# A two-layer decoder trunk on one core: the order of all engines' work laid by a timing model inside the kernel, in place of fixed distances

## The chip, the core and the metric

The kernel runs on one core of a Trainium2 chip. The core has a matrix engine (PE, with its weight loads shown as PEld), a vector engine (DVE), a scalar engine (ACT), a general engine (POOL), and a sync engine (SP) that issues most transfers. The metric is the device time of one execution in microseconds (us), as the median of several runs; lower is better.

## The reference, cut to what matters

Two layers over 256 tokens of width 1024, all in float32. Each layer is a half-step gated feed-forward (FFN) of inner width 2816, a token mixer beside a 4-head attention to 256 memory tokens, and a second half-step FFN; a last norm ends it. Layer 0's mixer is a causal pooling over windows of 2, 4, 8 and 16 tokens, layer 1's a differential attention with 8 heads.

```python
for i in range(2):
    kv = mem_n @ mem_w_kv[i]
    x = x + 0.5 * swiglu(rmsnorm(x, norm_g[i, 0]), ffn_w_up[i, 0], ffn_w_down[i, 0])
    h = rmsnorm(x, norm_g[i, 1])
    x = x + (pool_layer if i == 0 else diff_layer)(h, ..., mem_k, mem_v)
    x = x + 0.5 * swiglu(rmsnorm(x, norm_g[i, 2]), ffn_w_up[i, 1], ffn_w_down[i, 1])
return rmsnorm(x, final_norm_g)
```

## The kernel before

Every float32 product is made of three matmuls (`mm3`, L271): each operand is split into a rounded `hi` and a remainder `lo`, and hi*hi, hi*lo and lo*hi are summed in PSUM. Weights arrive as pieces of 1 MB (128 x 2048) into three `raw` buffers, issued by SP in one fixed queue (`Weights`). ACT casts each piece to `hi` (L244) and DVE subtracts to get `lo` (L248), in two halves each; four split pieces can be alive.

An FFN (`ffn`, L423) has 11 chunks `j` of 256 inner columns. `single(j)` is the first product: for both token tiles t, 24 matmuls of 512 columns into one of two `mm` PSUM banks. `gated(j, t)` follows it: ACT takes the Silu of the gate half (`s`, L437), DVE multiplies by the other half (`g`, L442); after the second tile PE transposes both (four `tr<-ident,g` matmuls, L279), ACT makes `gh` (L261) and DVE `gl` (L267). `down(j, t)` is the second product: 12 matmuls of 512 columns onto four `acc` banks. `steps` (L512) sets the order on PE: single 0, single 1, down 0, single 2, down 1 and so on, to single 9, down 8, single 10, and then down 9 and down 10 together, first for t=0 and then for t=1. In the first FFN (`begin`) downs come one chunk later (down 0 behind single 2), and chunk 2 goes to `acc` banks.

When an FFN ends, `close` transposes the new x for the next stage. The pooling mixer has four `pool_group` chains; `diff_consts` (L805) loads 128 copies of a small vector (`lp`) and makes constants of it through POOL, DVE (`dots`, L815) and ACT. The differential mixer has eight `diff_head` chains. Each goes PE (scores), DVE (`ds`, max), POOL (`nmx`, L853), ACT (exp), DVE (`dw`), PE (transposes), ACT (`wt`), PE (product with v), ACT (squares), POOL (`v`, `rs`, `comb`: L286, L287, L892), DVE (`on`, L896), PE (transposes), ACT, DVE.

Engines run in the order in which the program emits their instructions, PE, ACT, DVE and SP each its own. What sets that order is `Flow`: a counter `now` that is advanced by a fixed amount after each triple of matmuls (0.648), and chains that `yield` a fixed distance before their next step (`SLACK = 7.3` between the gating multiply and its transposes; tuples such as `HEAD`, `MEM`, `POOL`, `CLOSE` for the others). `F.finish` runs a chain to its end at once where its result is needed.

Of the kernel before, what the change touches and what calls it, by code (L numbers as in the profile page):

```python
# [18 lines left out]
P = 128  # L19
# [17 lines left out]
PACE = 1.2  # L37
HURRY = 0.8
AHEAD = 1
# [8 lines left out]
SLACK = 7.3  # L48
HOLD = {0: 28.5, 1: 30.5, 2: 36.5}
CLOSE_LATE = 3.0  # L50
CLOSE = (0.25, 1.75, 0.05, 0.05, 0.5)
EXP_AT = 0.6

HEAD = (0.05, 2.1, 2.1, 3.0, 0.15, 2.4, 0.2, 2.2, 2.55, 0.05, 0.45)
MEM = (2.6, 1.85, 0.45, 2.6, 0.5, 1.25, 3.45, 0.3, 0.05)
POOL = (0.75, 0.85, 3.5, 0.15, 0.75)
PAIR = (0.15, 0.9, 0.55, 0.75)
PAIR_SLACK = 3.0
COLS = (0.05, 1.5)
# [5 lines left out]

class Flow:
# [3 lines left out]
    def __init__(self):  # L70
        self.now = 0
        self.chains = []
        self.count = 0
        self.busy = False

    def add(self, chain, delay=0):
        self.count += 1
        self.chains.append((self.now + delay, self.count, chain))
        self.poll()
        return self.count  # L80
# [5 lines left out]
    def step(self):  # L86
        c = min(self.chains)
        self.chains.remove(c)
        self.now = max(self.now, c[0])
        self.busy = True  # L90
        try:
            self.chains.append((c[0] + next(c[2]), c[1], c[2]))
        except StopIteration:
            pass
        self.busy = False

    def spend(self, time):
        self.now += time
        self.poll()
# [6 lines left out]
class Weights:  # L106
# [17 lines left out]
    def pump(self):  # L124
# [20 lines left out]
        self.flow.add(self.next())  # L145

    def next(self):
        key, _, _, pre, post, frees = self.queue[self.started]
        raw, before = pre(self.raw) if pre else (self.raw.get(key), None)
        self.done[key] = yield from self.run(key, raw, before)  # L150
# [4 lines left out]
        self.started += 1  # L155
        self.running = False
# [13 lines left out]
def trunk(ctx, tc, I, out):  # L170
    nc = tc.nc
    cst = ctx.enter_context(tc.tile_pool(name="cst", bufs=1))
    wp = ctx.enter_context(tc.tile_pool(name="wp", bufs=WB))
    act = ctx.enter_context(tc.tile_pool(name="act", bufs=1))
    tmp = ctx.enter_context(tc.tile_pool(name="tmp", bufs=2))
    sm = ctx.enter_context(tc.tile_pool(name="sm", bufs=4))
    ps_acc = ctx.enter_context(tc.tile_pool(name="ps_acc", bufs=4, space=PSUM))
    ps_mm = ctx.enter_context(tc.tile_pool(name="ps_mm", bufs=2, space=PSUM))
    ps_tr = ctx.enter_context(tc.tile_pool(name="ps_tr", bufs=1, space=PSUM))
    ctx.enter_context(tc.manual_schedule(engines=ORDERED))  # L180
    F = Flow()
# [9 lines left out]

    def mm_bank():
        return ps_mm.tile([P, 512], F32, tag="mm", name=nm("mm"))

    turn = [0]

    def tr_bank():
        turn[0] ^= 1
        tag = ("tr", "tr2")[turn[0]]
        return ps_tr.tile([P, 512], F32, tag=tag, name=nm("tr"))  # L200

    def one_bank(tag):
        return ps_tr.tile([P, 512], F32, tag=tag, name=nm("tr"))
# [28 lines left out]

    def split_piece(key, raw, before):
        if not isinstance(key, tuple):
            yield from special[key](raw)
            return raw
        hi = wp.tile([P, PIECE], F32R, tag="hi", name=nm("hi"))
        lo = wp.tile([P, PIECE], F32R, tag="lo", name=nm("lo"))
        pace = PACE if len(W.done) >= AHEAD else HURRY
        for s in range(0, PIECE, SPLIT):  # L240
            sl = slice(s, s + SPLIT)
            if before is not None:
                nc.vector.tensor_add(raw[:, sl], raw[:, sl], before[:, sl])
            nc.scalar.copy(hi[:, sl], raw[:, sl])  # L244
            yield pace
        for s in range(0, PIECE, SPLIT):
            sl = slice(s, s + SPLIT)
            nc.vector.tensor_sub(lo[:, sl], raw[:, sl], hi[:, sl].bitcast(F32))  # L248
            if s + SPLIT < PIECE:
                yield pace  # L250
# [26 lines left out]
    def transposes(o, src, n):  # L277
        for i in range(n):
            nc.tensor.transpose(o[:, cols(i)], src[:, cols(i)], ident)  # L279
        F.now += 0.109 * n  # L280
# [15 lines left out]
    def row_rstd(rstd):  # L296
# [4 lines left out]
        r = sm.tile([P, SEQ], F32, tag="row", name=nm("row"), bufs=2)  # L301
        nc.vector.tensor_copy(r, b[:, 0:SEQ])
        return r
# [5 lines left out]
    make_identity(nc, ident)  # L309
# [16 lines left out]
    ready = [0, 0]  # L326
# [8 lines left out]
    def close(t, gain0):  # L335
        b = [None, None]

        def flip(h):
            b[h] = tr_bank()
            transposes(b[h], x[:, t, half(h)], 4)  # L340

        def scaled(h):
            c = t2k("xc").rearrange("p (k n) -> p k n", k=4)
            for k in range(4):
                g = gain0 + 4 * h + k
                nc.scalar.activation(c[:, k, :], b[h][:, cols(k)], AF.Copy, scale=gcol[:, g:g + 1])
            b[h] = c
# [5 lines left out]
        yield CLOSE[0] + CLOSE_LATE * t  # L353
        flip(0)
        yield CLOSE[1]
        scaled(0)
        yield CLOSE[2]
        flip(1)
        yield CLOSE[3]
        lo(0)  # L360
        scaled(1)
        yield CLOSE[4]
# [9 lines left out]
    def finish(t, ss, y):  # L372
# [5 lines left out]
        yield 1.6  # L378
# [6 lines left out]
    def proj_tok(hx, pcs, t, bank=mm_bank):  # L385

        if hx is xT:
            F.finish(ready[t])
        o = bank()
        for q in range(2):  # L390
            wh, wl = pcs[q]
            for k in range(4):
                kk = 4 * q + k
                mm3(o, hx[0][:, kk, cols(t)], hx[1][:, kk, cols(t)], wh[:, k, :], wl[:, k, :], kk == 0, kk == KT - 1)
                F.spend(0.648)
        return o

    def proj_feat(hx, pcs, c):

        if hx is xT:  # L400
            F.finish(*ready)
        o = mm_bank()[:, 0:SEQ]
        for kk in range(KT):
            wh, wl = [v[:, kk % 4, cols(c)] for v in pcs[kk // 4]]
            mm3(o, wh, wl, hx[0][:, kk, :], hx[1][:, kk, :], kk == 0, kk == KT - 1)
            F.spend(0.327)
        return o

    def accumulate(acc, t, lh, ll, pc, k0, first, end=None):

        for i in range(4):
# [3 lines left out]
            F.spend(0.648)  # L415
# [3 lines left out]
    def exp_table():  # L419
        nc.scalar.activation(dcol2, dcol, AF.Exp)  # L420
        yield 0

    def ffn(layer, f, end, begin=None, exp_next=False):  # L423
# [5 lines left out]
        def gate(o, t, dst):  # L429

            while t is not None and rstd[t] is None:
                yield 0.3
            s = t2k("s")[:, 0:FC]
            if t is None:
                nc.scalar.activation(s, o[:, 0:FC], AF.Silu)
            else:
                nc.scalar.activation(s, o[:, 0:FC], AF.Silu, scale=rstd[t])  # L437
# [630 lines left out]
```

## Time and profile before

| | us |
|---|---|
| median of 3 runs | 1060.48 |
| lowest, highest | 1059.52, 1062.87 |
| the profiled execution, its own time | 1060.8 |
| its span, first to last instruction | 1059.1 |
| PE busy, share of the span | 1034.4 (98%) |
| DVE busy, ACT busy, POOL busy | 581.2, 540.9, 58.7 |

The profile covers one execution; 1.7 us of its time lie outside the span. An engine's busy time is the union of its instructions' records. A matmul's record is longer than the distance to the next matmul, so a PE that is shown busy is fully loaded only where its instructions also follow at their usual distance. "[0.72 <-ACT gh L261]" behind an instruction is the idle time of its engine before it and what ended it.

### The profile page before, as it was taken

Reading aid. Unit: us, or ns where it says so; the run is one execution under the profiler, and the core shown is the slowest. Engines: PE = TensorE matmul, PEld = TensorE weight load, DVE = VectorE, ACT = ScalarE, POOL = GpSimd, SP = SyncE. Lnnn points to the kernel's source line nnn. Section 1 sums busy time; section 2 is a strip of 40 time slices with the busy share of each in tenths; the row PEclk is TensorE's granted clock in tenths of the full one; section 3 lists DMA queues with packets and bytes.
Section 4 is the critical chain, followed back from the end, with each engine's and each line's share of the span. In section 5 each row is a group of like instructions: output and inputs, shape, how many; then the busy total and the mean of one; then the engine's idle time right before and its main releaser. Section 6 shows DMA issues by size and latency. Waiting matters only on the chain.

```text
span 1059.1 us, 12948 instructions
## 1 busy us (share of the span) xinstructions
PE 1034.4 (98%) x5156; PEld 868.1 (82%) x5156; DVE 581.2 (55%) x794; ACT 540.9 (51%) x857; POOL 58.7 (6%) x129
## 2 busy tenths in 40 slices
PE   8999999989999999999999999899998999999997
PEld 7888887879888888887888888789997888888885
DVE  6555655455764445454545454536776764545454
ACT  6645645655566444344644453454656565445342
POOL 2000220200000000000000000010122000000000
PEclk9999999999999999999999999999999999999999
DMA  8747655434545454554454555525343544455541
GB/s 313 283 160 277 241 197 185 173 124 173 185 134 205 179 199 159 199 187 170 160 199 162 196 196 192 192 95 199 123 157 120 182 164 171 164 194 198 188 151 40
DMA packets 28396, 190.26 MB, mean 180 GB/s; under 512 B 3248, under 2 KB 3504, under 8 KB 6192
## 3 DMA queue, kind: packets, MB, share of 16 engines
q1 hardware_dynamic: 28048, 188.92, 48.6%
q8 instruction: 40, 0.66, 0.2%
q10 hardware_dynamic: 288, 0.52, 0.1%
q14 instruction: 20, 0.16, 0.0%
HBM read 188.38 MB, written 1.05 MB: 179 GB/s over the span
## 4 chain that ended last, share of the span: by engine, by line
PE 88%; DVE 4%; ACT 3%; DMA 2%; issue 1%; POOL 1%; SPq 0%; POOLq 0%; ACTq 0%; DVEq 0%
PE mm L273 18%; PE mm L275 18%; PE mm L274 18%; PE acc L275 10%; PE acc L273 9%; PE acc L274 9%; PE tr L279 3%; DVE lo L248 2%; ACT hi L244 1%; DMA raw<-in_ffn_w_up 1%; DMA raw<-in_ffn_w_down 0%; DMA lp<-in_diff_lambda 0%; ACT ds L861 0%; PE acc L842 0%; PE tr L687 0%
## 5 line engine op out<-in xcount | busy, mean ns | idle before, releaser
L244 ACT CAST hi<-raw 128x1024 fp32r<-128x1024 f32 x342 | 342.1, 1048 | 178.1 <-PE mm L275 78.8
L248 DVE TENSOR_TENSOR lo<-raw,hi 128x1024 fp32r<-128x1024 f32 x342 | 402.0, 1221 | 28.3 <-ACT hi L244 27.9
L273 PE MATMUL mm<-hi,xT 128*128 128x512 f32 x736 | 291.5, 396 | 0.2
L275 PE MATMUL mm<-hi,xT 128*128 128x512 f32 x736 | 287.5, 391 | 0.0
L274 PE MATMUL mm<-lo,xT 128*128 128x512 f32 x736 | 286.8, 390 | 0.0
L275 PEld LDWEIGHTS mm<-hi,xT 128*128 128x128 f32 x736 | 138.1, 188 | 30.5 <-DVE xT L267 1.3
L273 PEld LDWEIGHTS mm<-hi,xT 128*128 128x128 f32 x736 | 138.2, 188 | 27.9 <-ACT xT L261 0.9
L274 PEld LDWEIGHTS mm<-lo,xT 128*128 128x128 f32 x736 | 138.4, 188 | 27.6 <-DVE lo L248 0.3
L273 PE MATMUL acc<-hi,gh 128*128 128x512 f32 x352 | 139.7, 397 | 4.3 <-ACT gh L261 4.3
L275 PE MATMUL acc<-hi,gl 128*128 128x512 f32 x352 | 139.3, 396 | 2.5 <-DVE gl L267 2.5
L274 PE MATMUL acc<-lo,gh 128*128 128x512 f32 x352 | 138.7, 394 | 0.0
L267 DVE TENSOR_TENSOR gl<-tr,gh 128x512 fp32r<-128x512 f32 x44 | 30.4, 691 | 180.8 <-ACT gh L261 180.7
L442 DVE SCALAR_TENSOR_TENSOR g<-mm,rstd,s 128x256 f32<-128x256 f32 x84 | 40.4, 481 | 135.3 <-ACT s L437 135.3
L437 ACT ACTIVATE s<-mm,rstd 128x256 f32<-128x256 f32 x84 | 39.9, 475 | 95.1 <-PE mm L275 95.0
L273 PEld LDWEIGHTS acc<-hi,gh 128*128 128x128 f32 x352 | 66.9, 190 | 18.8 <-ACT gh L261 5.3
L275 PEld LDWEIGHTS acc<-hi,gl 128*128 128x128 f32 x352 | 67.2, 191 | 18.5 <-DVE gl L267 4.4
L274 PEld LDWEIGHTS acc<-lo,gh 128*128 128x128 f32 x352 | 67.1, 191 | 13.9
L261 ACT CAST gh<-tr 128x512 fp32r<-128x512 f32 x44 | 25.8, 586 | 103.0 <-PE tr L279 103.0
L273 PE MATMUL mm<-xT,hi 128*128 128x256 f32 x192 | 56.1, 292 | 1.1 <-DVE mq L267 1.1
L275 PE MATMUL mm<-xT,lo 128*128 128x256 f32 x192 | 54.5, 284 | 0.2 <-DVE lo L248 0.2
L274 PE MATMUL mm<-xT,hi 128*128 128x256 f32 x192 | 54.3, 283 | 0.0
L286 POOL TENSOR_SCALAR v<-ss 128x1 f32<-128x1 f32 (+1 forms) x24 | 7.1, 295 | 710.7 <-ACT junk L293 682.1
(175 smaller groups left out, 1043.4 us busy)
## 6 DMA issues: line engine op xcount, KB each, us to landing
raw<-in_ffn_w_up SPq DMA_DIRECT2D x86, 1024.0 KB, 4.8
raw<-in_ffn_w_down SPq DMA_DIRECT2D x44, 1024.0 KB, 5.0
raw<-in_diff_w_in SPq DMA_DIRECT2D x14, 1024.0 KB, 4.8
raw<-in_mem_w_kv SPq DMA_DIRECT2D x8, 1024.0 KB, 4.8
raw<-in_pool_w_in SPq DMA_DIRECT2D x6, 1024.0 KB, 4.7
raw<-in_pool_w_out SPq DMA_DIRECT2D x6, 1024.0 KB, 4.7
raw<-in_diff_w_out SPq DMA_DIRECT2D x6, 1024.0 KB, 4.7
raw<-in_ffn_w_up SPq DMA_DIRECT2D x8, 256.0 KB, 6.3
```

The costliest lines, as they stand in the source:

```text
L244: nc.scalar.copy(hi[:, sl], raw[:, sl])
L248: nc.vector.tensor_sub(lo[:, sl], raw[:, sl], hi[:, sl].bitcast(F32))
L261: nc.scalar.copy(hi, src)
L267: nc.vector.tensor_sub(lo, src, hi.bitcast(F32))
L273: nc.tensor.matmul(o, lh, rh, start=start, stop=False, skip_group_check=more)
L274: nc.tensor.matmul(o, lh, rl, start=False, stop=False, skip_group_check=more)
L275: nc.tensor.matmul(o, ll, rh, start=False, stop=stop, skip_group_check=more)
L279: nc.tensor.transpose(o[:, cols(i)], src[:, cols(i)], ident)
L286: nc.gpsimd.tensor_scalar(v, ss, 1.0 / n, eps, op0=ALU.mult, op1=ALU.add)
L437: nc.scalar.activation(s, o[:, 0:FC], AF.Silu, scale=rstd[t])
L442: nc.vector.scalar_tensor_tensor(dst, o[:, FC:2 * FC], rstd[t], s, op0=ALU.mult, op1=ALU.mult)
```

## The change

A `Clock` now holds, for each engine, when it comes free, and for each block of 64 elements of a tile when it was written and last read. Every instruction that the program emits is priced by a formula (`Engine.note`) and booked there. `F.now` is the modelled end of PE's work. A chain no longer yields a fixed distance: it yields `at(tile)`, the modelled time at which its input is there, and `+ MARGIN` (0.25) ahead of PE work. The two halves' `hi` and `lo` of a weight piece are emitted when the modelled backlog of ACT or DVE is under `BACKLOG` (0.3). The two PSUM banks for transposes are taken and given back (`take`, `give`) where they alternated.

Beside this: in the three later FFNs down 8 moves behind single 10, where it stood in the first already, and runs there for both tiles before downs 9 and 10 go tile by tile; the first FFN's other downs move up by one chunk, so that all four have one order; the gate writes Silu into the tile that the multiply then overwrites; the x tiles are loaded behind chunk 1's weights, not chunk 2's; the memory tokens, which the condition `js[-1] == 5` loaded and split twice (for single 5 and down 5), are loaded once. The distances at which heads and groups are started (`MEM_EVERY`, `POOL_EVERY`, `DIFF_EVERY`) stay.

```diff
-SLACK = 7.3
-HOLD = {0: 28.5, 1: 30.5, 2: 36.5}
-HEAD = (0.05, 2.1, 2.1, 3.0, 0.15, 2.4, 0.2, 2.2, 2.55, 0.05, 0.45)
+MARGIN = 0.25
+BACKLOG = 0.3
+class Clock:
+    SEEN = {"pe": 0.2, "dve": 0.08, "act": 0.08, "pool": 0.1, "sp": 0.0}
...
+    def run(self, engine, time, outs, ins, seen=None):
+        t = max(self.free[engine], self.ready(*ins), self.ready(*outs) - self.SEEN[engine])
...
+        self.free[engine] = t + time
+        self.mark(t + time, t + time + (self.SEEN[engine] if seen is None else seen), outs, ins)
...
+        if op == "dma_start":
+            c.free["sp"] = t = max(c.run("sp", 0.0, outs, ins, 0.0), c.free[self.name]) + 0.33
+            c.free["dma"] = t = max(t + 1.4, c.free["dma"]) + 4.0 * width(outs[0]) * P / 330e3
...
+            if op == "transpose":
+                time = 0.109
+            elif ins[0].dtype == F32R:
+                time = max(0.12, n * 17 / 16 / 2400)
...
+        elif self.name == "dve":
+            time = (151 + n) / 960
+        elif self.name == "act":
+            time = (224 + n) / 1200 + (0.19 if len(outs) > 1 else 0)
+        else:
+            time = 0.1 + 0.0021 * n
...
         def gated(j, t, o, other):
             g = t2k("g")[:, 0:FC]
-            yield 0.15
             yield from gate(o, t, g)
...
-            yield SLACK
-            if begin and j in HOLD:
-                yield max(0, HOLD[j] - F.now)
-            F.finish(other)
+            yield from F.over(other)
             part_tiles(j)
-            b = one_bank("tr")
+            yield at(*[gts[j, i] for i in range(NT)]) + MARGIN
+            b = yield from take()
             for i in range(NT):
                 transposes(b[:, cols2(i)], gts[j, i], 2)
...
+                downs(*js[:-2])
                 for t in range(NT):
-                    for i in js:
+                    for i in js[-2:]:
...
-        lag = 2 if begin else 1
-        order = [("single", j) for j in range(lag - 1, lag)]
-        for j in range(lag, NJ):
-            order += [("single", j), ("down", j - lag)]
-        return order[:-1] + [("down", *range(NJ - 1 - lag, NJ))]
+        order = [("single", j) for j in range(1 if begin else 0, 2)]
+        for j in range(2, NJ):
+            order += [("down", j - 2), ("single", j)]
+        return order[:-2] + [("single", NJ - 1), ("down", NJ - 3, NJ - 2, NJ - 1)]
...
         nc.sync.dma_start(lp, I["diff_lambda"].to_broadcast([P, 4, 64]))
-        yield 4.0
+        yield at(lp)
...
-        yield 1.0
+        yield at(pr)
         nc.vector.tensor_reduce(dots, pr, axis=AX.X, op=ALU.add)
...
         nc.gpsimd.tensor_tensor(comb, rs, r3[:, :, 0], op=ALU.mult)
-        yield HEAD[7]
+        yield at(comb)
         on = t2k("on")[:, 0:SEQ].rearrange("p (a b) -> p a b", a=NT)
         for t in range(NT):
             nc.vector.tensor_scalar(on[:, t, :], o[:, cols(t)], comb[:, t:t + 1], None, op0=ALU.mult)
-        yield HEAD[8]
-        b = tr_bank()
+        give(o)
+        yield at(on) + MARGIN
+        b = yield from take()
         transposes(b, on.rearrange("p a b -> p (a b)"), 2)
...
-            if begin and kind == "single" and js[0] == 2:
-                W.add("x", I["x"].rearrange("b (t p) d -> p (b t) d", p=P), "none")
-            if begin and js[-1] == 5:
+            if begin and kind == "single" and js[0] == 1:
+                W.add("x", I["x"].rearrange("b (t p) d -> p (b t) d", p=P), "none", frees=())
+            if begin and kind == "single" and js[0] == 5:
                 W.add("cols", I["mem_cols"])
                 W.add("mem", I["mem"].rearrange("b (t p) d -> p (b t) d", p=P))
```

## Rows read from the trace of the kernel before

**Rows 1.** Waits of PE: engine, line waited for: us in total, times, longest us.

```profile
PE acc L273 <- ACT gh L261: 4.3, 4, 2.2
PE acc L275 <- DVE gl L267: 2.5, 2, 1.6
```

**Rows 2.** Windows: stretch, us, busy us and instructions by engine, PE's granted clock.

```profile
237.30:240.72 3.42, 3.42 (x19) 3.42 (x18) 3.12 (x6) 2.00 (x5) 0.00 (x0) 0.50 0.15 19
330.00:489.00 159.00, 159.00 (x722) 131.58 (x721) 80.47 (x88) 70.62 (x87) 0.00 (x0) 1.00 0.51 190
493.30:496.70 3.40, 3.40 (x9) 2.65 (x9) 0.69 (x1) 0.00 (x0) 0.00 (x0) 0.50 1.00 417
684.40:691.30 6.90, 5.98 (x15) 4.35 (x14) 2.65 (x4) 0.00 (x0) 0.00 (x0) 0.51 0.68 283
740.00:812.00 72.00, 69.16 (x569) 64.26 (x569) 51.97 (x156) 45.82 (x132) 15.47 (x29) 1.00 0.38 139
```

**Rows 3.** Timeline of PE at the ends of the second and third FFN.

```profile
489.15 0.39 PE L275 MATMUL acc<-hi,gl 128*128 128x512 f32 x1
489.38 0.60 PE L279 MATMUL tr<-ident,g 128*128 128x128 f32 x4
490.70 0.50 PE L273 MATMUL acc<-hi,gh 128*128 128x512 f32 x1 [0.72 <-ACT gh L261]
...
493.04 0.59 PE L275 MATMUL acc<-hi,gl 128*128 128x512 f32 x1 [1.61 <-DVE gl L267]
...
683.97 0.50 PE L273 MATMUL acc<-hi,gh 128*128 128x512 f32 x1 [2.23 <-ACT gh L261]
...
685.73 0.80 PE L275 MATMUL acc<-hi,gl 128*128 128x512 f32 x1 [0.92 <-DVE gl L267]
```

**Rows 4.** Timeline of ACT at the end of the third FFN.

```profile
678.62 0.47 ACT L437 ACTIVATE s<-mm,rstd 128x256 f32<-128x256 f32 x1 [1.62 <-PE mm L275]
```

**Rows 5.** Timelines of SP, POOL, DVE and PE around the constants' load.

```profile
229.68 0.43 SPq L807 DMA_DIRECT2D lp<-in_diff_lambda  x1
...
234.53 0.59 POOL L813 TENSOR_TENSOR pr<-lp 128x64 f32<-128x64 f32 x2 [26.56 <-DMA lp<-in_diff_lambda]
...
235.16 0.28 DVE L815 TENSOR_REDUCE dots<-pr 128x2 f32<-128x128 f32 x1 [5.92 <-POOL pr L813]
...
236.09 0.39 PE L274 MATMUL tr<-pl,hi 128*128 128x256 f32 x1 [3.91 <-DVE pl L267]
```

**Rows 6.** Timeline in the differential heads.

```profile
785.63 1.22 DVE L248 TENSOR_TENSOR lo<-raw,hi 128x1024 fp32r<-128x1024 f32 x1
785.80 1.13 POOL L853 TENSOR_SCALAR nmx<-mx 128x4 f32<-128x4 f32 x1 [6.81 <-DVE mx L850]
...
797.88 0.89 POOL L286 TENSOR_SCALAR v<-ss 128x2 f32<-128x2 f32 x1 [4.45 <-ACT junk L888]
...
799.87 0.61 DVE L896 TENSOR_SCALAR on<-tr,comb 128x128 f32<-128x128 f32 x2 [1.15 <-POOL comb L892]
...
800.53 0.44 PE L279 MATMUL tr<-ident,on 128*128 128x128 f32 x2 [1.35 <-DVE on L896]
```

**Rows 7.** Timelines of PE, SP and ACT at the start.

```profile
18.76 0.39 PE L273 MATMUL mm<-hi,xT 128*128 128x512 f32 x1
...
20.50 0.90 SPq L226 DMA_DIRECT2D x_res<-in_x  x2
...
27.21 1.05 ACT L293 ACTIVATE junk<-x_res 128x1024 bf16<-128x1024 f32 x1
```

**Rows 8.** DMA issues: transfer, queue, count, KB each, us to landing.

```profile
raw<-in_mem_cols SPq DMA_DIRECT2D x2, 1024.0 KB, 5.0
```

**Rows 9.** Timelines of DVE and PE in the body of the second FFN.

```profile
336.16 0.48 DVE L442 SCALAR_TENSOR_TENSOR g<-mm,rstd,s 128x256 f32<-128x256 f32 x1 [0.63 <-ACT s L437]
...
344.96 0.60 PE L279 MATMUL tr<-ident,g 128*128 128x128 f32 x4
```

More of the change, by code (lines that the diff above doesn't have):

```diff
@@ L66, with __init__ @@
 class Flow:
-    def __init__(self):
-        self.now = 0
+    def __init__(self, clock):
+        self.clock = clock
+        self.least = 0.0
         self.chains = []
@@ L74, in __init__, with now @@
         self.busy = False
+    @property
+    def now(self):
+        return max(self.least, self.clock.free["pe"])
     def add(self, chain, delay=0):
         self.count += 1
-        self.chains.append((self.now + delay, self.count, chain))
+        number = self.count
+        self.chains.append((self.now + delay, number, chain))
         self.poll()
-        return self.count
+        return number
     def poll(self):
@@ L95, in step, with until, over @@
         self.busy = False
-    def spend(self, time):
-        self.now += time
-        self.poll()
+    def until(self, true):
+        while not true():
+            self.step()
+    def over(self, *which):
+        while any(c[1] in which for c in self.chains):
+            yield self.now + 0.1
     def finish(self, *which):
@@ L144, in pump, with first, second @@
         self.running = True
-        self.flow.add(self.next())
-    def next(self):
-        key, _, _, pre, post, frees = self.queue[self.started]
+        self.flow.add(self.first(self.queue[self.started]))
+    def first(self, entry):
+        key, _, _, pre, _, _ = entry
         raw, before = pre(self.raw) if pre else (self.raw.get(key), None)
-        self.done[key] = yield from self.run(key, raw, before)
+        rest = yield from self.run(key, raw, before)
+        self.started += 1
+        self.running = False
+        self.flow.add(self.second(entry, rest))
+        self.pump()
+    def second(self, entry, rest):
+        key, _, _, _, post, frees = entry
+        self.done[key] = yield from rest
         if post:
@@ L190, in acc_bank, with take, give, take_now @@
         return ps_acc.tile([P, 512], F32, tag="acc", name=nm("acc"))
+    read_later = set()
+    mm_names = []
     def mm_bank():
[L193 to L203, printed above, removed]
+        if len(mm_names) >= 2:
+            F.until(lambda: mm_names[-2] not in read_later)
+        t = ps_mm.tile([P, 512], F32, tag="mm", name=nm("mm"))
+        mm_names.append(t.name)
+        return t
+    taken = set()
+    def take():
+        while len(taken) == 2:
+            yield F.now + 0.1
+        tag = min((tag for tag in ("tr", "tr2") if tag not in taken), key=lambda tag: last_use.get(tag, 0.0))
+        taken.add(tag)
+        t = ps_tr.tile([P, 512], F32, tag=tag, name=nm("tr"))
+        held[t.name] = tag
+        yield at(t)
+        return t
+    held = {}
+    last_use = {}
+    def give(t):
+        tag = held.pop(t.name)
+        taken.discard(tag)
+        last_use[tag] = clock.used(t)
+    def take_now():
+        while len(taken) == 2:
+            F.step()
+        asked = take()
+        try:
+            while True:
+                next(asked)
+        except StopIteration as e:
+            return e.value
     def raw_tile(tag="raw"):
@@ L231, in load, with idle @@
         return raw
+    def idle(engine):
+        return clock.free[engine] - BACKLOG
     def split_piece(key, raw, before):
@@ L325, in trunk @@
     rows = [None]
-    ready = [0, 0]
+    closed = set()
     dcol2 = cst.tile([P, 1], F32, name="dcol2")
@@ L338, in flip @@
         def flip(h):
-            b[h] = tr_bank()
+            b[h] = yield from take()
             transposes(b[h], x[:, t, half(h)], 4)
@@ L599, in mem_stats @@
         for t in range(NT):
+            yield max(at(m[:, t, :]), idle("act"))
             mem_rstd.append(rstd_of(sumsq(m[:, t, :]), D, EPS, "mrstd"))
-            yield COLS[1]
-        F.chains.append((F.now + 3.0, -1, mem_rows()))
+        F.add(mem_rows())
     def mem_rows():
-        mem_row.append(row_rstd(mem_rstd))
-        yield 0
+        yield at(*mem_rstd) + MARGIN
+        mem_row.append(row_rstd((yield from take()), mem_rstd, cst.tile([P, SEQ], F32, name="mem_row")))
     gains = []
```

324 lines of the change are left out of this document (206 added, 118 removed).

## The prediction, made before the changed kernel was run

> **What bounds the kernel now.** I read the waits of PE first, then the windows, then PE's timeline where a wait stands. In the body of an FFN PE is the bound and nothing else is: over 159 us it has no idle time at all, with DVE busy for half of it and ACT for less [rows 2]. There the distance of two 512-column matmuls is 0.23 us, and a record of 0.39 us reaches 0.16 us into the next [rows 3]; so the work of PE itself is fixed, and the change takes nearly none of it away. What can be won is PE's waiting. The listed waits of PE are few and long: `gh` four times, `gl` twice [rows 1], and once `pl` [rows 5]. The same is true of the granted clock: three stretches show 0.50 or 0.51, which is 1.2 instead of 2.4 GHz, and each comes right behind, or inside, one of these waits [rows 2, 3, 5]. So the question is which of the waits the new order removes, and where it makes new ones.
>
> **The ends of the FFNs.** The last chunk's transposes go out only when `F.finish` forces them, directly before the matmuls that need them. PE then waits for ACT's cast and DVE's subtraction. An idle time in a row hides the 0.16 us that the record reaches over, so a wait is its idle time plus 0.16. Second FFN: 0.72 and 1.61 give 0.88 and 1.77; third: 2.23 and 0.92 give 2.39 and 1.08 [rows 3]. The other two of the four waits for `gh` share 4.3 - 0.72 - 2.23 = 1.35 us [rows 1], 0.67 each, so 0.83 each, in the first and fourth FFN. Sum 7.8 us. Behind the change the last chunk's chain starts at the same place, the end of single 10, but PE has down 8 (24 matmuls of 0.23, 5.5 us) and the first tile of down 9 (12, 2.8 us) before it needs the result: 8.3 us. The slowest such chain of before ran from the Silu at 678.62 [rows 4] to the matmul at 685.73 [rows 3], 7.1 us, with a table load in it that the model doesn't price. It fits. I take all 7.8; the lower bound is 5, if the third FFN keeps most of its 3.5.
>
> **The clock.** Three stretches at half clock hold 19 matmuls of 256 columns in 3.42 us, 9 of 512 in 3.40 us and 15 of 512 in 6.90 us [rows 2]. At 0.23 us for 512 and 0.12 for 256 these are 2.3, 2.1 and 3.5 us of work: 1.1, 1.3 and 3.4 lost, of which 1.08 in the third is the wait already counted. That is 4.7 us; half of PE's busy time in them is 6.4. I take 5.4. The rows show the drop only behind waits, so without the waits it should go; if small waits elsewhere bring it back, it stays (rival two).
>
> **The constants' load.** `dots` sits in DVE's queue 5.92 us for POOL's `pr`, and `pr` for the load that SP could issue only at 229.68 [rows 5]. The subtraction `pl` is queued behind it, and PE waits 3.91 + 0.16 = 4.1 us for `pl`. The model knows that SP is late, so it emits `dots` later. But it lands the load 0.33 + 1.4 + 0.4 = 2.1 us after the issue and lets POOL take 0.5, together 2.7 with the signals; the trace has 235.16 - 229.68 = 5.5. So DVE still blocks for up to 2.8 us, somewhat later. Before, a block of 5.9 became a wait of 4.1: 1.8 were covered. With the same cover 2.8 leaves 1.0. Gain 3.1, between 1.3 (no cover) and 4.1.
>
> **The heads.** From 740 to 812 PE idles 72.00 - 69.16 = 2.8 us [rows 2]. Here the new prices are wrong in one place: any small POOL instruction costs 0.1. The trace has `v` starting at 797.88 and `on` at 799.87, with `rs` and `comb` between: 2.0 us [rows 6]; the model books 0.4. `on` goes into DVE's queue 1.6 us too early, and its transposes into PE's after 0.25 of margin and on average half a triple of 256-column matmuls, 0.18. If DVE has nothing else, PE waits 1.15 us. DVE is busy 51.97 of 72 us, 0.72 of the time [rows 2], mostly with subtractions of 1.22 [rows 6], and where one stands before `on` the wait lies inside it: 0.72 x 0.61 = 0.44 off. So 0.7 us for each of eight heads, 5.6 us, against 2.8 before: a loss of 2.8. The bounds are 0 and 16 (2.0 for each head, as in the row). The other chains are priced well: the Silu's 0.47 and the multiply's 0.48 [rows 4, 9] are 0.40 and 0.42 in the model plus 0.08 for the signal. ACT's exps and DVE's maxima have no error that a margin would not hold.
>
> `nmx` shows the same fault from another side: it took 1.13 us and ended at 786.93, 0.08 us after the subtraction beside it (785.63 + 1.22) [rows 6]. The Trainium skill, "SBUF — State Buffer", section "SBUF: two separate sides", says that a DVE instruction with two SBUF inputs and a GpSimd instruction that reads SBUF exclude each other for the whole instruction. By that rule, the trace agrees, and each POOL step of a head could cost up to one subtraction more; this speaks against the change, and rival two prices it from the rows.
>
> **The rest.** The transposes in the body of the FFNs lose their cushion: before, `g` ended at 336.64 and they started at 344.96, 8.3 us later [rows 9]; now the model's moment plus 0.25. Its errors there are under 0.2 us (ACT's casts start a signal's delay after PE's release, which the model leaves out), less than the margin, and PE has other work queued. I book 0, bounds 0 and 44 x 0.6 (rival three). At the start single 1 runs from 18.76 [rows 7] for 48 x 0.23 = 11 us, and down 0 now follows at 29.8, a chunk earlier. Its gate needs the squares of x, which started at 27.21 with x issued at 20.50 [rows 7]. Two pieces of 1 MB are no longer ahead of x: at 5.0 us to landing for one alone [rows 8], and less when two follow each other, x is there 5 to 8 us earlier, by 19 to 22, and two squares of 1.05 [rows 7], statistics, gate and transposes, an estimated 6 us, end before 29.8. I book a loss of 0.3, bounds 0 and 3. The memory tokens' second load [rows 8] costs no path: DMA, ACT and DVE have room there. Four transposing records of PE, 0.5 us with a short wait, go with it. Silu's shared tile, the earlier x rows, the taken banks and the closings change queues with idle engines behind them: 0; if that cover were gone it would be tenths at each of four seams.
>
> **Sum.** 7.8 + 5.4 + 3.1 + 0.5 - 2.8 - 0.3 = 13.7 us from the profiled 1060.8 gives 1047.1; that execution lies 0.3 over the median, so 1046.8.
>
> **Rivals.** One: the heads become clean too, because DVE's queue always covers POOL, and the load's and the start's losses don't appear. For it: DVE's 0.72. Against: PE waited 1.35 for `on` although the fixed distances were wider [rows 6]. Then 1046.8 - 5.6 - 1.0 - 0.3 = 1039.9.
>
> Two: the heads cost 2.0 us each, by POOL's 2.0 us and by subtractions excluding it. For it: `v` 0.89 and `nmx` 1.13. Against: such lengths hold only where a subtraction stands beside. 16 instead of 5.6 gives 1057.2; a clock drop in there would add 1 to 3.
>
> Three, the other side: the missing cushion. If the model places the FFN's 44 sets of transposes too early by more than margin and spacing of the triples hold, PE waits each time, in a stretch that has no wait now. It eats the gain at 13.7/44 = 0.31 us for each set, and makes the kernel slower by over 0.3% at 0.38. At 0.6, one cast of ACT (1.05) half in the way, 26 us: 1073. Against it: the body repeats every 17 us (72 matmuls of 0.23), so one error shows in all or none, and the priced times agree with the rows.
>
> Four: the new order is in effect the old one and the waits only move, from the end of an FFN to single 10, which now follows single 9 directly and wants four weight pieces in a row. Against: PE takes a piece in 5.5 us in either order. 1058 to 1062.
>
> **Chances.** Forecast 0.58 (1041 to 1052), one 0.15, two 0.13, three 0.08, four 0.06. A measurement of this kernel tells 0.3%, 3.2 us, from no change. Faster by more: the forecast, one, 0.10 of two and 0.01 of four, 0.84. Within: 0.03 of two and 0.05 of four, 0.08. Slower: three, 0.08. The range leaves out three, four and the worst of two above, and the best of one below: 1037 to 1057, under 2 in 10.
>
> **What would show it.** Right: no wait of PE for `gh` or `gl` behind the last chunk's transposes; granted clock 1.00 throughout but for the last microseconds; DVE's idle time before `dots` under 3 us; `mem_cols` once; PE's idle time in the heads 4 to 8 us, released by `on`. Wrong: waits of PE in front of `tr<-ident,g` in the bodies (three), a clock of 0.50 in the heads (two), or PE waiting for `hi` or `lo` in single 10 (four).

## The result, and the profile after

The changed kernel takes 1036.34 us (median of 4, 1035.53 to 1036.77), the kernel before 1061.34 in the same comparison (median of 4, 1059.52 to 1062.87). The ratio is 0.9764, its 95% interval 0.9746 to 0.9783: 25 us less, where 13.7 were forecast, and 0.7 us below the lower end of the range. The profiled execution of the changed kernel has a span of 1034.3 us at a mean granted clock of 0.999, against 1059.1 at 0.992.

All instructions of the changed kernel go through the helper at line 144, so every row carries L144 and is read by its tile. The page's busy times and chain that ended last:

```profile
PE 1022.5 (99%) x5152; PEld 863.5 (83%) x5152; DVE 587.3 (57%) x785; ACT 535.5 (52%) x845; POOL 55.1 (5%) x125
...
PE 98%; DMA 1%; ACT 0%; DVE 0%; POOL 0%; SPq 0%; issue 0%; POOLq 0%; ACTq 0%
```

PE is busy 11.9 us less, with four records fewer out of 5156, and idle 12.9 us less. So half of the gain is waiting and half is the same matmuls at a higher clock and a closer distance. The waits of PE after, all that are listed (engine, line waited for: total, times, longest):

```profile
PE acc L144 <- ACT xT L144: 2.5, 1, 2.5
PE tr L144 <- DVE on L144: 1.1, 2, 0.7
PE tr L144 <- DVE warm L144: 1.1, 1, 1.1
```

The waits for `gh` and `gl` [rows 1] and the one for `pl` [rows 5] are gone. The windows after (stretch and length; busy time and instructions of PE, PEld, DVE, ACT and POOL; PE's granted clock; share and GB/s of DMA; in order the body of the second FFN, its end, the end of the third, the heads):

```profile
318.00:470.00 152.00, 152.00 (x691) 125.81 (x690) 78.41 (x84) 66.17 (x82) 0.00 (x0) 1.00 0.54 193
470.00:490.40 20.40, 20.40 (x98) 16.88 (x97) 11.92 (x14) 12.44 (x22) 0.00 (x0) 1.00 0.43 155
657.00:677.10 20.10, 20.10 (x96) 16.62 (x96) 11.90 (x14) 13.87 (x24) 0.00 (x0) 1.00 0.45 157
720.00:792.00 72.00, 70.88 (x579) 66.01 (x578) 52.87 (x159) 48.58 (x139) 14.36 (x32) 1.00 0.36 127
```

Both ends are without an idle moment and at clock 1.00, where [rows 2] had 0.50 and 0.51. In the heads PE idles 1.1 us in 72 where it idled 2.8: I had forecast 5.6.

To place the gain I cut PE's timeline at the last second-product matmul of each FFN and at the last output-product matmul of the pooling and differential blocks. A stretch is the time from one of these cuts to the next, in us; the first starts at the first matmul, at 1.1 in both:

| stretch | before | after | difference |
|---|---|---|---|
| first FFN | 195.40 | 193.57 | -1.83 |
| pooling | 114.91 | 108.97 | -5.95 |
| second FFN | 191.76 | 186.71 | -5.05 |
| third FFN | 193.68 | 186.72 | -6.96 |
| differential | 167.25 | 164.19 | -3.07 |
| fourth FFN | 187.59 | 185.79 | -1.80 |

### The profile page after: what moved, and what is told of

Read it like the earlier page. It is cut to its first block, busy times and chain, and to the rows that moved or that the text cites. A ratio compares the mean times of both kernels' runs of the same rounds, so it can differ in the third digit from the quotient of the medians.

```text
span 1034.3 us, 12976 instructions
## 1 busy us (share of the span) xinstructions
PE 1022.5 (99%) x5152; PEld 863.5 (83%) x5152; DVE 587.3 (57%) x785; ACT 535.5 (52%) x845; POOL 55.1 (5%) x125
## 3 DMA queue, kind: packets, MB, share of 16 engines
HBM read 186.29 MB, written 1.05 MB: 181 GB/s over the span
## 4 chain that ended last, share of the span: by engine, by line
PE 98%; DMA 1%; ACT 0%; DVE 0%; POOL 0%; SPq 0%; issue 0%; POOLq 0%; ACTq 0%
PE mm L144 61%; PE acc L144 32%; PE tr L144 5%; DMA x_cols<-in_x_cols 1%; ACT junk L144 0%; SPq L144 0%; POOL rs L144 0%; DVE x_res L144 0%; DVE on L144 0%; ACT raw L144 0%; DVE raw L144 0%; POOL v L144 0%; POOLq L1252 0%; ACT xT L144 0%; DVE cat_lo L144 0%
## 5 line engine op out<-in xcount | busy, mean ns | idle before, releaser
L144 DVE TENSOR_TENSOR lo<-raw,hi 128x1024 fp32r<-128x1024 f32 (+1 forms) x350 | 414.8, 1211 | 245.0 <-ACT hi L144 244.3
L144 PE MATMUL mm<-hi,xT 128*128 128x512 f32 x1504 | 474.2, 391 | 0.0
L144 ACT CAST hi<-raw 128x1024 fp32r<-128x1024 f32 (+1 forms) x350 | 352.1, 1038 | 203.9 <-PE mm L144 137.8
L144 PEld LDWEIGHTS mm<-hi,xT 128*128 128x128 f32 x1504 | 282.4, 188 | 58.2
L144 PE MATMUL mm<-lo,xT 128*128 128x512 f32 x752 | 292.8, 389 | 0.0
L144 PEld LDWEIGHTS mm<-lo,xT 128*128 128x128 f32 x752 | 141.3, 188 | 28.9
L144 PE MATMUL acc<-hi,gh 128*128 128x512 f32 x352 | 141.1, 401 | 0.0
L144 PE MATMUL acc<-hi,gl 128*128 128x512 f32 x352 | 137.7, 391 | 0.0
L144 PE MATMUL acc<-lo,gh 128*128 128x512 f32 x352 | 137.3, 390 | 0.0
L144 ACT ACTIVATE g<-mm,rstd 128x256 f32<-128x256 f32 x86 | 40.3, 468 | 118.6 <-PE mm L144 118.6
L144 DVE SCALAR_TENSOR_TENSOR g<-mm,rstd,g 128x256 f32<-128x256 f32 x86 | 41.4, 481 | 89.0 <-ACT g L144 89.0
L144 PEld LDWEIGHTS acc<-hi,gl 128*128 128x128 f32 x352 | 66.1, 188 | 14.3
L144 PEld LDWEIGHTS acc<-lo,gh 128*128 128x128 f32 x352 | 66.3, 188 | 12.5
L144 PEld LDWEIGHTS acc<-hi,gh 128*128 128x128 f32 x352 | 66.2, 188 | 12.4
L144 PE MATMUL mm<-xT,hi 128*128 128x256 f32 x384 | 72.2, 288 | 0.0
L144 PEld LDWEIGHTS mm<-xT,hi 128*128 128x128 f32 x384 | 59.6, 191 | 1.3 <-issue 1.0
L144 ACT CAST gh<-tr 128x512 fp32r<-128x512 f32 x44 | 25.8, 587 | 59.9 <-PE tr L144 59.9
L144 POOL TENSOR_SCALAR v<-ss 128x1 f32<-128x1 f32 (+1 forms) x24 | 9.8, 410 | 853.3 <-ACT junk L144 853.3
L144 PE MATMUL mm<-xT,lo 128*128 128x256 f32 x192 | 54.3, 283 | 0.0
L144 DVE TENSOR_TENSOR gl<-tr,gh 128x512 fp32r<-128x512 f32 x44 | 30.4, 692 | 26.1 <-ACT gh L144 26.1
L144 PE MATMUL acc<-hi,cat_hi 128*128 128x512 f32 x96 | 38.5, 401 | 0.0
L144 PE MATMUL acc<-lo,cat_hi 128*128 128x512 f32 x96 | 37.5, 391 | 0.0
```

The lines of the kernel that those rows point to most:

```text
L144: return call(*args, **kwargs)
```

## The experiments

Stretches are those of the table; "span" is that of the profiled execution (1059.1 before, 1034.3 changed), and times are medians. The kernel before was timed anew beside each set of runs, with medians from 1061.1 to 1062.7, so a gain in medians can be up to 2 us larger than one in spans; the readings below go by stretches.

**One part alone, put into the kernel before.** The edits:

```diff
 b_consts
-        yield 4.0
+        yield 12.0
 b_close
-CLOSE_LATE = 3.0
+CLOSE_LATE = 1.0
 b_slack
-SLACK = 7.3
+SLACK = 2.5
 b_group
-        return order[:-1] + [("down", *range(NJ - 1 - lag, NJ))]
+        cut = 1 if begin else 3
+        return order[:-cut] + ([] if begin else [("single", NJ - 1)]) + [("down", NJ - 3, NJ - 2, NJ - 1)]
...
+                downs(*js[:-2])
                 for t in range(NT):
-                    for i in js:
+                    for i in js[-2:]:
```

b_consts emits `dots` and what follows it 8 us later.

> The kernel before with one edit: the reduction dots is emitted 8 us later, so that DVE no longer blocks ahead of pl. Theory (every wait of PE is worth itself and the half-clock stretch behind it): the wait of 4.1 us and 1.1 to 1.3 us of clock go, 5.2 to 5.4 us less. Rival (the block only moves onto the next chain, as the prediction's 1.0 us of rest supposed): 3 to 4 us less.

1054.57 us, ratio 0.9923 (0.9904 to 0.9942); the pooling stretch is 5.65 us shorter. The whole wait and its half clock are gained, as the theory says (5.2 to 5.4), and not the 4.2 of my sum. In medians it is 8.2 us: 1.6 us of it is the second FFN, whose half clock was absent here without an edit (see the last section). The same window of the two kernels, before and then b_consts:

```profile
229.00:246.00 17.00, 13.09 (x97) 12.89 (x96) 9.40 (x17) 5.82 (x11) 2.01 (x4) 0.90 0.40 134
```

```profile
229.00:246.00 17.00, 17.00 (x145) 17.00 (x143) 12.11 (x22) 8.83 (x16) 3.84 (x9) 1.00 0.54 194
```

> The kernel before with the regrouped last second products alone (down 8 behind single 10 in the three later FFNs), fixed distances kept. Theory: the gate's steps and SLACK make 8.75 us, the new cover is 8.2, so the transposes are still forced directly before their use and a wait of at least 0.8 us stays at each end; but ACT and DVE have had time to empty, so the long waits (1.77, 2.39, 1.08) shrink: 3 to 6 us less with the clock. Rival one (the regrouping itself is what pays): 9 to 12 us less. Rival two (it does nothing without the model): within 1 us.

1052.73 us, 0.9906 (0.9883 to 0.9928), span -7.3: the second FFN -3.23, the third -5.16. These two stretches give 8.4 us and the medians 10.0, more than the 3 to 6 expected, and the medians lie where rival one put them (9 to 12). The theory is right in the waits. Those for `gl` are gone, those for `gh` are still four, but short:

```profile
PE acc L273 <- ACT gh L261: 2.7, 4, 0.7
```

> The kernel before with SLACK 2.5 instead of 7.3, order of the products kept. Theory: the first FFN alone has cover enough (5.4 us against 3.95), so about 1 us less; the other three still force their transposes. Rival (a smaller distance costs waits in the bodies, where 44 sets lose their cushion): 5 us or more slower.

1053.56 us, 0.9919 (0.9892 to 0.9946). The profiled execution, with span -3.7, was the slowest of four (1057.15 us). The expected 1 us fell: the second FFN has -3.22 and the third -4.57, nearly as much as the regrouping gives. But the short distance is too short once, in the first FFN (+2.87 in this execution): transposes of `g`, ready at 39.5 us, wait until the `gl` before them has read the PSUM bank that they write, at 42.4:

```profile
PE tr L279 <- DVE gl L267: 2.8, 1, 2.8
PE acc L273 <- ACT gh L261: 2.6, 3, 1.3
```

> The kernel before with both edits, regrouped last products and SLACK 2.5. Theory: all four ends lose their waits and the two half-clock stretches: 7.8 plus 4 to 4.6 us of clock, 11 to 12.5 us less. Rival (fixed distances cannot place them, only the model can): under 6 us less.

With both edits: 1048.22 us, 0.9864 (0.9845 to 0.9883), span -12.0, as expected. No wait for `gh` is left and one of 0.4 for `gl`; the stretches are -1.04, +1.05, -4.42, -6.35, +0.04, -1.20 (the +1.05 is a longer half clock behind the wait for `pl`, which is still there). Either edit alone leaves part of the wait: the chain has to start early and the matmuls in front of its use have to be there.

> The kernel before with CLOSE_LATE 1.0 instead of 3.0: the second tile's closing transposes go out 2 us earlier. Theory (the prediction's zero for the closings was wrong: at each start of an FFN PE loses some 0.6 us to a closing that is forced): 0.4 to 0.6 us at each of four seams, 1.5 to 2.5 us less. Rival (the closings cost nothing): within 0.5 us.

1059.49 us (median of 10), 0.9989 (0.9979 to 0.9999), span -2.0. The total can't settle so little: in the other stretches half clocks came and went (pooling +1.16, the second FFN -2.13). The fourth FFN, where nothing else differs, has -0.62. The place is behind the second closing transposes of a seam, the passage from one block to the next. PE of the kernel before, first microseconds of the fourth FFN:

```profile
868.42 0.60 PE L279 MATMUL tr<-ident,x_res 128*128 128x128 f32 x4
868.77 0.48 PE L273 MATMUL mm<-hi,xT 128*128 128x512 f32 x1
...
870.25 0.60 PE L279 MATMUL tr<-ident,x_res 128*128 128x128 f32 x4
870.90 0.50 PE L273 MATMUL mm<-hi,xT 128*128 128x512 f32 x1
871.24 0.40 PE L274 MATMUL mm<-lo,xT 128*128 128x512 f32 x1
871.63 0.50 PE L275 MATMUL mm<-hi,xT 128*128 128x512 f32 x1
871.97 0.39 PE L273 MATMUL mm<-hi,xT 128*128 128x512 f32 x1
```

The first matmul follows the first set of transposes after 0.35 us, but the second set after 0.65, and two more follow after 0.39 and 0.34 in place of 0.23. That is 0.57 us in which the page shows PE nearly busy throughout, and it is in no list of waits.

**All of it with fixed distances.** b_all is the kernel before with the five edits that need no model: the four above and the memory tokens loaded once. b_head adds one to the distance ahead of the heads' last transposes:

```diff
 b_head, on top of b_all (HEAD[8])
-HEAD = (0.05, 2.1, 2.1, 3.0, 0.15, 2.4, 0.2, 2.2, 2.55, 0.05, 0.45)
+HEAD = (0.05, 2.1, 2.1, 3.0, 0.15, 2.4, 0.2, 2.2, 4.2, 0.05, 0.45)
```

> The kernel before, fixed distances kept, with five small edits together: regrouped last products, SLACK 2.5, dots 8 us later, the memory tokens loaded once, CLOSE_LATE 1.0. Theory (the waits are what is won, whoever places the work): 12 for the ends, 5.5 to 6.5 for the constants, 0.5 to 1 for the second load, about 2 for the closings, 20 to 22 us less, so within 3 to 5 us of the changed kernel, the rest lying in the heads. Rival (the model places much more than these waits): 10 us or more slower than the changed kernel.

1040.25 us, 0.9807 (0.9792 to 0.9822), span -20.6. The second, third and fourth FFN take 186.72, 186.72 and 185.78 us, the changed kernel's to 0.02. Of the 4.2 us that are missing, 3.2 lie in the differential stretch, 0.3 in pooling, 0.7 in the first FFN.

> The kernel before with the five edits together and the heads' last distance, from `on` to its transposes, 4.2 instead of 2.55. Theory (the rest between the fixed distances and the model are the waits for `on`, 1.6 us, and little else): 1.5 to 2 us less than with the five edits, in the differential stage alone. Rival (later transposes push the heads' end into the output product): no gain or a loss.

1047.2 us, 0.9864 (0.9845 to 0.9883). Not better but worse, as the rival said, though by another way: the differential stretch is 7.4 us longer than b_all's. The two waits for `on` themselves are gone; in all eight heads the transposes of `on` now start 0.8 us or more after it ended. The two waits that the list puts down to `on` are those of transposes of `dw`, which don't read it. What the two share is a PSUM bank: here the two banks for transposes alternate, and the product that `on` reads lies in one of them until `on` has run. So the longer distance seems to have changed whose turn meets a bank still in use; the turns themselves weren't traced. The clock falls inside the first of these waits (waits of PE, the first of them, then a window of the heads, granted clock 0.77):

```profile
PE tr L279 <- DVE on L898: 4.4, 2, 2.9
PE tr L279 <- DVE dw L871: 1.4, 1, 1.4
```

```profile
748.62 0.90 PE L279 MATMUL tr<-ident,dw 128*128 128x128 f32 x3 [2.92 <-DVE on L898]
```

```profile
745.00:760.00 15.00, 10.60 (x65) 10.19 (x66) 9.62 (x24) 7.31 (x20) 3.21 (x7) 0.77 0.26 86
```

The changed kernel takes and gives these banks instead. So b_head doesn't show that fixed distances can't reach it: fixed distances with taken banks weren't run, nor other distances.

**One part undone in the changed kernel.**

```diff
 a_oldorder
         for j in range(2, NJ):
             order += [("down", j - 2), ("single", j)]
+        if not begin:
+            return order + [("down", NJ - 2, NJ - 1)]
 a_twice
-            if begin and kind == "single" and js[0] == 5:
+            if begin and js[-1] == 5:
...
 a_early
-MARGIN = 0.25
+MARGIN = -1.0
 a_m05
-MARGIN = 0.25
+MARGIN = 0.5
```

> The changed kernel with the three later FFNs' products in the old order (down 8 ahead of single 10), timing model kept. Theory: cover of one tile of down 9, 2.8 us, against a chain of 3.5 to 4.5 us from the end of single 10: a wait of about 1 to 1.5 us at each of three ends, 3 to 5 us slower than the changed kernel, no clock drop. Rival (the regrouping carries the gain at the ends): 8 us or more slower.

1040.99 us, 0.9809 (0.9794 to 0.9823), span +4.5 to the changed kernel: the second FFN +1.27, the third +2.45, the fourth 0. These 3.7 us lie within the 3 to 5 expected, though at two ends and not three; the other 0.86 is a half clock at the start (see the last section). The model alone doesn't clear the ends; waits for `gh` come back:

```profile
PE acc L144 <- ACT gh L144: 1.9, 2, 1.2
PE acc L144 <- DVE gl L144: 0.6, 1, 0.6
```

> The changed kernel with the memory tokens loaded and split twice again. Theory: four more transposing records of PE and little else, 0.4 to 0.6 us slower. Rival (the second splitting crowds ACT and DVE, and the order in the first FFN suffers): 1 us or more slower.

1036.8 us, 0.9773 (0.9757 to 0.9789), span +0.8, of it 0.71 in the first FFN. Of that 0.5 appears at the four added transposes (108.8 us), as booked, and 0.2 lies in the first ten microseconds, ahead of the second load.

> The changed kernel with MARGIN -1.0 instead of 0.25: transposes and the like are emitted 1.25 us earlier than the modelled moment of their input. Theory (the model's moment is right to within the margin, so PE now waits what it comes too early, less what falls on the spacing of the triples): 0.5 to 1.0 us at each of 44 chunks and some more in the heads, 25 to 50 us slower. Rival (the body has cushion of its own, the margin does not matter): under 5 us slower.

1080.49 us, 1.0186 (1.017 to 1.0201), span +44.4. This is rival three, made to happen:

```profile
PE tr L144 <- DVE g L144: 21.9, 41, 0.5
```

These are 41 waits of half a microsecond. With 4.9 us for `on` (1.1 in the changed kernel) and some short ones, the listed waits grow by 28 us; the other 16 are in distances between matmuls that the list doesn't count. The price of the rival, 0.6 us a set, was about right: the four FFNs are 31.2 us longer, 0.71 for each of 44 sets. Its condition isn't met at 0.25: in the changed kernel `g` ended at 329.97 and its transposes start at 330.46, and its list of waits has none for `g`.

```profile
329.49 0.48 DVE L144 SCALAR_TENSOR_TENSOR g<-mm,rstd,g 128x256 f32<-128x256 f32 x1
```

```profile
330.46 0.60 PE L144 MATMUL tr<-ident,g 128*128 128x128 f32 x4
```

> The changed kernel with MARGIN 0.5 instead of 0.25. Theory (0.25 already holds the model's errors in the bodies; more delay only moves work into room that PE does not need): within 1 us. Rival (a part of the transposes comes too early even with 0.25): 2 us or more faster.

1035.63 us, 0.976 (0.9746 to 0.9775): no change that can be measured, with -0.66 in the differential stretch and +0.55 in the first FFN's start.

**The prices of the heads.** The forecast's largest error lies there, so five kernels went to it.

```diff
 a_s5: POOL's small statistics at the trace's price
-            time = 0.1 + 0.0021 * n
+            time = (0.5 if n == 2 else 0.1) + 0.0021 * n
 a_right: the other prices of a head as traced, POOL's left low
-                time = n * 4 / 2400
+                time = n * 4 / 2400 * (0.67 if ins[0].shape[0] == 64 else 1)
-            time = (151 + n) / 960
+            time = (151 + n) / 960 * (0.83 if op == 'tensor_tensor_reduce' else 1)
-            time = (224 + n) / 1200 + (0.19 if len(outs) > 1 else 0)
+            time = (224 + n) / 1200 + ((0.12 if outs[0].name.startswith('ds') else 0.19) if len(outs) > 1 else 0)
 a_late: five more, not priced by the model, behind comb
+        for _ in range(5):
+            nc.real.gpsimd.tensor_tensor(comb, rs, r3[:, :, 0], op=ALU.mult)
```

a_right_s5 has the first two together; a_s5_m05 has a_s5's edit and a margin of 0.5.

> The changed kernel with the heads' three POOL instructions v, rs and comb priced at 0.5 us each in the model, 1.5 in all, as the trace has them, instead of 0.1. Theory (the low price is what the two waits for on come from): the two waits go, 1.0 to 1.5 us less. Rival (the order in the heads is set by other queues): no change, or other waits in their place.

1035.13 us, 0.9753 (0.9738 to 0.9768), the differential stretch -0.86. The waits for `on` are gone; one for `mq` of 0.6 is left. So the wrong price costs one microsecond, not five.

> The changed kernel with the heads' score products, maxima and exps priced as the trace has them (0.86 instead of 1.28 us, 1.19 instead of 1.43, 1.87 instead of 2.15 for each head), POOL left at its low price. Theory one (these too long prices made up for POOL's): with them gone, `on` and its transposes come up to 0.9 us earlier in each of eight heads, and 2 to 6 us of waits for `on` appear. Theory two (DVE's queue ahead of `on` covers POOL by itself): within 1 us.

1037.38 us, 0.9768 (0.9753 to 0.9784). Here I had thought that other prices, too high, make up for POOL's. With them set right the heads should have got worse by microseconds; the differential stretch is 0.30 longer, the waits for `on` shrink from 1.1 to 0.2, and one of 1.0 for `mq` appears. That theory falls. (The span is 1.5 longer, nearly all of it in the first 14 us; see the last section.)

> The same with POOL's v, rs and comb priced at 0.5 us each too. Both theories: the waits for `on` go; theory one: about as fast as the changed kernel with POOL's price alone mended, 0.5 to 1.5 us less than the changed kernel. A rival: right prices everywhere leave no slack for what varies (nmx 0.2 to 1.1 us), and waits for `dw` or `on` of 1 us or more stay.

1034.51 us, 0.9744 (0.9728 to 0.976), the differential stretch -1.77, no listed wait but those at the start.

> The changed kernel with comb computed five times more on POOL, not booked in the model: on comes some 1.0 to 1.3 us later than now in each of eight heads. Theory (DVE's queue and the spacing of PE's work cover part of it; worked out from each head's idle time of DVE before on and the distance from on to its transposes): 3 to 5 us slower. Rival, the prediction's pricing (what POOL adds beyond the margin reaches PE): 8 to 10 us slower.

1043.52 us, 0.983 (0.9814 to 0.9847), 7.2 more than the changed kernel and so between what both sides expected: the total decides nothing. (The span is 8.0 longer, 0.9 of it a half clock at the start.) The reason is that the added work took 5 x 0.27 = 1.36 us a head, more than either had reckoned: 10.9 us for eight. The differential stretch grew by 6.84, 63% of that. The waits say where it went:

```profile
PE tr L144 <- DVE on L144: 5.4, 5, 1.8
PE mm L144 <- DVE mq L144: 1.0, 1, 1.0
```

> The changed kernel with the three POOL prices mended and MARGIN 0.5. Theory: no listed wait of PE but the start's is left in the heads, 0.9 to 1.5 us less than the changed kernel. Rival (the two edits mend the same waits): no faster than with the prices alone.

1034.22 us (1033.94 to 1034.31), 0.974 (0.9722 to 0.9758), span 1032.4, the differential stretch -1.62. It has the lowest median of the study, ahead of both; a_right_s5's times overlap it. Its ratio's interval overlaps the changed kernel's a little; the two ranges of times don't.

## Why the prediction was off

The direction and the places were right: the waits at the ends of the FFNs, their half clock and the constants' load. The size was off by 11.1 us of span, 24.8 against 13.7. By steps:

**The heads: the step that failed (5.9 us).** I forecast a loss of 2.8 and measured a gain of 3.07. What I said of POOL holds. From the end of ACT's last square to the end of `comb` the chain takes 1.3 to 2.0 us in the changed kernel where the model books 0.4, and DVE stood idle for it in five of the eight heads:

```profile
DVE on L144 <- POOL comb L144: 5.8, 5, 2.4
```

The step that failed is the cover that I set against POOL's lateness: 0.25 + 0.18 us ahead of PE's transposes and 0.44 in DVE's queue, the same in every head, which left PE a wait of 0.7 in each, 5.6 in all. PE waited 1.1 in all, none of it in six of the eight heads. Two heads in a row show both cases, DVE first and then PE:

```profile
751.64 0.61 DVE L144 TENSOR_SCALAR on<-tr,comb 128x128 f32<-128x128 f32 x2 [1.15 <-POOL comb L144]
...
754.05 0.61 DVE L144 TENSOR_SCALAR on<-tr,comb 128x128 f32<-128x128 f32 x2 [1.21 <-POOL comb L144]
```

```profile
752.94 0.38 PE L144 MATMUL tr<-ident,on 128*128 128x128 f32 x2
...
754.72 0.44 PE L144 MATMUL tr<-ident,on 128*128 128x128 f32 x2 [0.69 <-DVE on L144]
```

DVE waits about as long in both. In the first, `on` ends at 752.25 and PE comes to the transposes 0.69 us later, since other matmuls stand ahead of them in its queue; in the second PE is there first. Call this time from the end of `on` to the start of its transposes the room. Over the eight heads the transposes start 1.03, 1.49, 0.69, 0.06, 0.05, 1.45, 0.76 and 0 us after the end of `on`, and PE waits only 0.69 and 0.43, in the fourth and the eighth.

This distribution also prices a_late: 1.36 us more in each head, less this room, is 0.3 + 0 + 0.7 + 1.3 + 1.3 + 0 + 0.6 + 1.4 = 5.6. There PE's idle time before them was 0.04, 0, 0.40, 1.45, 1.23, 0, 0.51 and 1.80 us, 4.3 more in all than in the changed kernel, in the heads with little room or none; with the one for `mq` that is 5.3 of the 6.84. So a mean over covers was the mistake; the room stands in the program's own order, and is above a microsecond in some heads and nothing in others. What each stretch of that room consists of (a triple already emitted, a wait for a bank of PSUM, DVE work booked ahead of `on`) wasn't taken apart. That it isn't a balance of wrong prices is shown by a_right.

Nor does the gain of 3.07 come from `on` alone. The kernel before had these waits in the stretch:

```profile
PE tr L279 <- DVE on L896: 1.6, 2, 1.4
PE mm L273 <- DVE mq L267: 1.1, 1, 1.1
```

The changed kernel has 1.1 left for `on` and none for `mq`, which is 1.6 us; the rest lies in distances between matmuls. I subtracted all 2.8 us of idle time before without asking what it was. Which part of the change does this (the chains' moments, the rule for the pieces, the taken banks) no run separates.

The Trainium skill, "SBUF — State Buffer", section "SBUF: two separate sides", says that a GpSimd instruction that reads SBUF and a DVE instruction with two SBUF inputs keep each other out for their whole length. The trace agrees: the third head's `v` ran from 749.65 to 750.54 and DVE's subtraction, from 749.27, ended at 750.49; the next head's `v`, with no subtraction beside it, took 0.19 us.

```profile
749.27 1.22 DVE L144 TENSOR_TENSOR lo<-raw,hi 128x1024 fp32r<-128x1024 f32 x1
```

```profile
749.65 0.89 POOL L144 TENSOR_SCALAR v<-ss 128x2 f32<-128x2 f32 x1 [7.10 <-ACT junk L144]
...
752.78 0.19 POOL L144 TENSOR_SCALAR v<-ss 128x2 f32<-128x2 f32 x1 [1.18 <-ACT junk L144]
```

This lengthens the chain that the room above covers; rival two, in which it decides, didn't come about.

**The closings, booked at 0 (1.9 us).** The second, third and fourth FFN's stretches equal the sum of two experiments, b_group_slack and 0.62 for the closing: -4.42 - 0.62 = -5.04 (measured -5.05), -6.35 - 0.62 = -6.97 (-6.96), -1.20 - 0.62 = -1.82 (-1.80). My "tenths at each of four seams" was near the size, at three seams (pooling shows none), but I held it for covered since I searched the list of waits. The lost time stood in the distance of matmuls.

**The constants' load (1.75 us).** The pooling stretch gained 5.95, where 3.1 and 1.1 of clock were forecast. That the model "lands the load 0.33 + 1.4 + 0.4 = 2.1 us after the issue" was wrong, since I left out half of the formula in the diff: `max(t + 1.4, c.free["dma"])`. The load is issued 0.38 us behind a piece of 1 MB, on the same queue, so the model lets it land behind that one. SP, POOL and DVE of the changed kernel:

```profile
219.33 0.33 SPq L144 DMA_DIRECT2D raw<-in_pool_w_in  x1
219.71 0.43 SPq L144 DMA_DIRECT2D lp<-in_diff_lambda  x1
```

```profile
225.00 0.60 POOL L144 TENSOR_TENSOR pr<-lp 128x64 f32<-128x64 f32 x2 [21.77 <-DMA lp<-in_diff_lambda]
```

```profile
224.42 1.66 DVE L144 SCALAR_TENSOR_TENSOR cat_lo<-tr,gcol,cat_hi 128x256 fp32r<-128x256 f32 x4
225.99 0.28 DVE L144 TENSOR_REDUCE dots<-pr 128x2 f32<-128x128 f32 x1
```

The load takes 5.3 us to POOL's start, much as before (4.85 in [rows 5]), but `dots` now stands in DVE's queue behind work that lasts until then. The residual of 1.0 doesn't exist. The other 0.75 is half clock and small distances: b_consts gives 5.65 for a wait of 4.1, so 1.5 where I had 1.1, and 0.3 came with other parts of the change.

**The ends and the clock (0.75 us).** For the second and third FFN I had 2.65 + 3.47 of waits and 3.6 of clock, and the rounding up of 0.7: 10.4. b_group_slack gives 10.8. The first and fourth gave 1.04 and 1.20, not 0.83: the matmuls behind a short wait keep a longer distance, too (0.34 to 0.39 us). Both terms are right in mechanism. But I gave all the credit to the regrouping, with a chain that starts "at the same place"; the earlier start of the chain and the regrouping each give most of it alone.

**The start (0.8 us).** The first FFN gained 1.83, where 0.83 + 0.5 - 0.3 was forecast. The loss of 0.3 wasn't seen; `x` is in time, and PE's one wait at the start, 2.5 us for ACT's `xT`, was 2.2 before. The second load is worth 0.5, as booked, and the end of this FFN more than 0.83 (above). The rest is of the size by which the start differs between executions.

**The rivals.** One, clean heads, was nearest, at 1039.9; it lacked the closings and the whole of the load. Two and four left no trace. Three is real at a margin of -1.0 and absent at 0.25. (Its threshold is a little off: 44 sets of 0.38 make the kernel 3.0 us slower, not 3.2.)

## What to carry to other kernels

Most of what a planned order gives can be a few waits that a trace names: here five small edits of the fixed distances brought 20.6 of 24.8 us. The other 3 us, in a stretch whose steps interleave differently in each head, came with the model and the taken banks together; the one longer distance tried in their place cost 7, and no other was tried. A price that is wrong in such a model costs only what it exceeds the room in front of the consumer, so read that room instance by instance, not as a mean. Look for lost time in the distance of equal instructions as well as in the list of waits.

## What the runs showed of the hardware

Half clock behind one and the same wait lasts differently. Behind the 3.9 us wait for `pl` it was 3.42 us in the kernel before [rows 2] and about twice that, 6.8, in b_group, with the same instructions there and nearly the same wait, 3.8 (clock 0.80 over these 17 us against 0.90 above):

```profile
229.00:246.00 17.00, 13.24 (x92) 13.04 (x92) 9.43 (x15) 5.66 (x11) 2.01 (x4) 0.80 0.37 132
```

Behind the second FFN's waits of 0.72 and 1.61 it was 3.4 us in the kernel before, and absent in b_consts and b_close, which change nothing there and have the same idle time. The kernel before and b_consts, which is six microseconds ahead by then:

```profile
489.00:500.00 11.00, 8.67 (x37) 6.57 (x36) 5.37 (x6) 3.28 (x8) 0.00 (x0) 0.84 0.50 191
```

```profile
483.00:494.00 11.00, 8.67 (x43) 6.72 (x42) 6.58 (x8) 4.82 (x12) 0.00 (x0) 1.00 0.50 191
```

So one to two microseconds beside any of these waits come and go without an edit at that place.

The start does the same. The same first instructions ran at 1.00 in the changed kernel and at 0.50 in a_right, changed kernel first:

```profile
10.50:13.80 3.30, 3.30 (x15) 2.36 (x14) 2.04 (x5) 1.91 (x5) 0.00 (x0) 1.00 1.01 367
```

```profile
10.50:13.80 3.30, 3.30 (x9) 2.52 (x8) 2.00 (x5) 1.87 (x5) 0.00 (x0) 0.50 1.06 360
```

Fifteen matmuls against nine in 3.3 us: a difference of about 1.2 us in the first FFN's stretch that is no part of the edit. It is why differences under a microsecond were read from the stretch that an edit touches, not from the total.
